# Splitting the last operands by token halves, five sum banks and a new order of the first blocks at the entrance of the up projections of a hybrid decoder on one Trainium2 core

## Chip, cores and metric

The kernel runs on one core of a Trainium2 chip, as a single program. The core has a matrix engine (PE, with its weight loads listed as PEld), a vector engine (DVE), an activation engine (ACT), a general engine (POOL) and a queue that issues transfers (SP). The metric is the device time in microseconds (us), the median of several runs.

## The reference

A decoder of two layers works on 1040 tokens (16 learned meta tokens and 1024 others) of width 1024, in float32. Layer 0 has an SSD mixer, layer 1 stick-breaking attention. After each mixer comes the same gated feed-forward part, and the change lies where the two meet:

```python
h = h + hg @ w_out                     # layer 0: end of the mixer
h = h + o @ sb_w_o[j]                  # layer 1: end of the attention
h = h + _conv_ffn(_rmsnorm(h, ffn_norm[layer]), ...)

def _conv_ffn(u, w_up, conv_w, conv_b, w_down):
    h = _causal_dwconv(u @ w_up, conv_w, conv_b)      # 1024 -> 2 * 2816, three taps
    g, val = jnp.split(h, 2, axis=-1)
    return (jax.nn.silu(g) * val) @ w_down
```

## The kernel before

**Layout.** Activations lie with features on the 128 partitions and tokens along the free dimension: the stream `h` is eight tiles of 128 x 1040. Such wide tiles come from one pool of 28 buffers (`self.Q`, `NQ = 28`, line 25 to 27). A second pool holds twelve short buffers (`ft`, line 756), a third eight (`tmp`). The eight PSUM banks belong to four names: `mm` 2, `sm` 3, `lg` 2, `ex` 1.

**Products.** A float32 product is made of three passes over a high and a low part (`mm3`, line 150): high by high, high by low, low by high. So each operand is split first: ACT copies the high part, and DVE (activations, `split`, line 157) or POOL (weights, `load_w`, line 135) subtracts it to get the low part. `split` does a wide tile in three pieces of 348, 348 and 344 tokens, and its two results take two wide buffers.

**Entrance of the feed-forward part.** `out_proj` (layer 0) and `o_proj` (layer 1) add the mixer's product to `h`. All but the last four operands (layer 0), or the last two (layer 1), are added over the whole rows first; in layer 1 the operands 4 and 5 are added there for the first half of the tokens only. The rest goes through `enter_ffn` (line 714), in four token tiles of 260: `tile(j)` makes eight sums (`accumulate`, line 363: PE into a PSUM bank, then DVE adds the bank to `h`). Their banks are `mm`, `mm`, `ex` in turn, three in all. After tiles 0 and 1 come the factors of the norm for them (`factors`: squares on ACT, sums on POOL and DVE, a product with ones on PE, then Ln, Exp and four instructions of DVE). The weights of the last operands lie partly in the buffers `fh` and `fl` (two each) which the up projection's weights use too.

**Forms.** The up projection is a Winograd variant of Strassen's scheme with seven products in place of eight, over two token tiles at a time: a token pair `t` is 520 tokens (t = 0: tiles 0 and 1; t = 1: tiles 2 and 3). `forms` (line 759) makes its seven operands from the normed `h`, for k = 0 to 3: four scalings on DVE, four subtractions on POOL (all of t = 0; for t = 1 on POOL only where k is 2 or 3, else on DVE), and seven splits (ACT copies, DVE subtracts). Each of the seven forms takes two wide buffers, so one token pair takes 14. The forms are made in the order 1, 5, 0, 2, 3, 4, 6.

**Blocks.** `up` (line 821) runs over 22 blocks of 128 gate and 128 value features. `up_weights` (line 793) loads 1 MB for a block and makes its four weight operands f1 to f4 on ACT and POOL: three differences of 1024 columns, one of 512, and four sums of 512. f2 and f3 lie in the two buffers of `fh` and `fl`, f1 and f4 in three of `wh` and `wl`. A block on one token pair is seven products (0, 2, 3, 1, 4, 5, 6) of twelve matmuls each, with the additions between them, the convolution and the gate on ACT and DVE. Block 0 runs on pair 0, while the factors and forms of pair 1 (`rest`) are made, and then on pair 1; from block 1 on the products of both pairs alternate.

**Order.** Outside of two stretches with an order written by hand (the mixer, and PE in the attention) a planner orders each engine's instructions: of those ready by its own estimate of time, the one written first in the program goes first. The order is fixed before the run, and each engine then works through its list.

Of the kernel before, what the change touches and what calls it, by code (L numbers as in the profile page):

```python
# [8 lines left out]
F32 = mybir.dt.float32  # L9
F32R = mybir.dt.float32r  # L10
AF = mybir.ActivationFunctionType
ALU = mybir.AluOpType

P = 128
# [4 lines left out]
L = META + SEQ  # L19
# [5 lines left out]
QW = 1056  # L25
# [5 lines left out]
FN = 260  # L31
HB = 2
# [8 lines left out]
KF = FF // P  # L41
PAIRS = 8
# [26 lines left out]
class Trunk:  # L69
# [87 lines left out]
    def split(self, t, s, eng=None):  # L157

        nc = self.nc
        hi, lo = self.Q(s + "h", F32R), self.Q(s + "l", F32R)  # L160
        for s0, n in TT:
            c = slice(s0, s0 + n)
            nc.scalar.activation(hi[:, c], t[:, c], AF.Copy)
            (eng or nc.vector).tensor_tensor(lo[:, c], t[:, c], hi[:, c].bitcast(F32), op=ALU.subtract)
        return hi, lo

    def ln_exp(self):
# [192 lines left out]
            self.nc.gpsimd.tensor_copy(t[:, :front], self.zero[:, :front])  # L360
        return t

    def accumulate(self, h, f, s0, n, w, ks, front=0, bank=None):

        ps = (bank or (self.ex if f % 3 == 2 else self.mm))("acc")
        c, o = slice(s0, s0 + n), slice(front + s0, front + s0 + n)
        for i, (hi, lo) in enumerate(ks):
            wh, wl = w(i, f)
            self.mm3(ps[:, :n], wh, wl, hi[:, c], lo[:, c], i == 0, i == len(ks) - 1)
        self.nc.vector.tensor_tensor(h[f][:, o], h[f][:, o], ps[:, :n], op=ALU.add)  # L370
# [324 lines left out]
    def out_proj(self, hd, ys, yd, pool):  # L695

        a = self.a
        h = [None] * KD
        for g in range(3):
            ops = [self.split(ys[g][q] if yd[g] is None else self.fetch(yd[g][q], "y"), "y") for q in range(4)]  # L700
            for f in range(KD):
                w = self.load_w(a["w_out_f"][g, f], 4 * P)
                if g == 0:
                    h[f] = self.fetch(hd[f], "h", front=HB)
                for s0, n in TT:
                    self.accumulate(h, f, s0, n, lambda i, f: (w[0][:, i * P : i * P + P], w[1][:, i * P : i * P + P]), ops, HB)
        ops = [self.split(ys[3][q], "y") for q in range(4)]
        ws = [self.load_wd(a["w_out"][12 + i], pool if i < 2 else None) for i in range(4)]
        return self.enter_ffn(0, h, [(ws, ops)] * 2, pool)

    def load_wd(self, src, pool):
        return self.load_w(src, D, pool=pool, tags=("fh", "fl") if pool else ("wh", "wl"))
# [1 line left out]
    def enter_ffn(self, layer, h, last, pool):  # L714


        nc = self.nc
        r = self.rp.tile([P, QW], F32, tag="r", name=self.nm("r"))
        nc.gpsimd.tensor_copy(r[:, :HB], self.zero[:, :HB])
        d = self.dp.tile([KD, P, L], F32, tag=f"hm{layer}", name=f"hm{layer}")  # L720
        def sums_of(j):
            c = slice(HB + FN * j, HB + FN * j + FN)
            return self.square_sum([x[:, c] for x in h], FN, D), r[:, c]

        def tile(j, work):
            ws, ops = last[j // 2]
            for f in range(KD):
                self.accumulate(h, f, FN * j, FN, lambda i, f: (ws[i][0][:, f * P : f * P + P], ws[i][1][:, f * P : f * P + P]), ops, HB)
                if f % 2:
                    next(work, None)  # L730

        def factors(j):
            sums, c = sums_of(j)
            self.rstd(sums, FN, D, c, j % 2 == 0)

        def rest():
            for j in (2, 3):
                factors(j)
            for k in range(KD):
                nc.sync.dma_start(d[k], h[k][:, HB : HB + L])  # L740
            yield from self.forms(h, r, 1, f"ffn_norm{layer}", forms[1], pool)

        forms = [{i: (self.Q("bh", F32R), self.Q("bl", F32R)) for i in (1, 5, 0, 2, 3, 4, 6)} for _ in range(2)]
        for j in (0, 1):
            tile(j, iter(()))
            factors(j)
        w0 = self.up_weights(layer, 0, pool)
        work = self.forms(h, r, 0, f"ffn_norm{layer}", forms[0], pool)
        tile(2, work)
        tile(3, work)  # L750
        for _ in work:
            pass
        return d, w0, forms, rest()
# [67 lines left out]
    def up(self, layer, w0, forms, rest, pool):  # L821

        nc = self.nc
        tt = nc.vector.tensor_tensor
        N = HB + FN
        cw, cb = f"ffn_conv_w{layer}", f"ffn_conv_b{layer}"
        d = self.dp.tile([KF, P, L], F32, tag=f"g{layer}", name=f"g{layer}")

        def block(b, t, w):

            def product(i, ps, start=True):
                wh, wl, c0 = w[i]
                hi, lo = forms[t][i]
                for k in range(KD // 2):
                    c, e = slice(c0 + k * P, c0 + k * P + P), slice(k * FW, k * FW + N)
                    self.mm3(ps[:, :N], wh[:, c], wl[:, c], hi[:, e], lo[:, e], start and k == 0, k == KD // 2 - 1, not start)
                return ps

            def conv(x, i, c):
                o = self.tmp("c")
                self.conv(x, o[:, :FN], FN, 3, HB, lambda q: self.par(cw, (KF * i + b) * 3 + q), self.par(cb, KF * i + b))
                if i == 0:
                    nc.scalar.activation(o[:, :FN], o[:, :FN], AF.Silu)
                return o

            def done(g, v, j):
                tt(g[:, :FN], g[:, :FN], v[:, :FN], op=ALU.mult)
                nc.sync.dma_start(d[b, :, FN * j : FN * j + FN], g[:, :FN])  # L850

            def copy(ps):
                s = self.ft(pool)
                nc.scalar.activation(s[:, :N], ps[:, :N], AF.Copy)
                return s

            add = lambda o, x, y: tt(o[:, :N], x[:, :N], y[:, :N], op=ALU.add)
            x = product(0, self.mm("p"))
            p1 = copy(x)
            yield  # L860
            y = product(2, self.sm("p"))
            add(y, y, p1)
            u2 = copy(y)
            yield
            z = product(3, (self.ex if next(turn) else self.lg)("p"))
            p5 = copy(z)
            add(z, z, u2)
            yield
            g0 = conv(product(1, x, False), 0, 0)
            yield  # L870
            u3 = copy(product(4, y, False))
            add(p5, p5, u3)
            v1 = conv(p5, 1, 1)
            yield
            done(conv(product(5, z, False), 0, 1), v1, 2 * t + 1)
            yield
            done(g0, conv(product(6, y, False), 1, 0), 2 * t)
            yield

        turn = cycle((0, 0, 1))  # L880
        for b in range(KF):
            w = self.up_weights(layer, b, pool) if b else w0
            s, t = (block(b, t, w) for t in range(2))
            if b:
                for _ in zip(s, t):
                    pass
            else:
                next(rest)
                for _ in s:
                    next(rest, None)  # L890
                for _ in t:
                    pass
        return d

    def down(self, layer, gd, hd, pool, after):
# [347 lines left out]
    def o_proj(self, hd, od, pool):  # L1243

        a = self.a
        h = [None] * KD
        first = PAIRS - 2
        ops = [self.split(self.fetch(od[p], "o"), "o") for p in range(first)]
        for f in range(KD):
            w = self.load_w(a["w_o_f"][f], first * P)  # L1250
            h[f] = self.fetch(hd[f], "h", front=HB)
            for j in range(4):
                self.accumulate(h, f, FN * j, FN, lambda i, f: (w[0][:, i * P : i * P + P], w[1][:, i * P : i * P + P]), ops[: first if j < 2 else first - 2], HB)
        ops = ops[first - 2 :] + [self.split(self.fetch(od[p], "o"), "o") for p in range(first, PAIRS)]
        ws = [self.load_wd(a["w_o"][first - 2 + i], pool if i < 2 else None) for i in range(4)]
        return self.enter_ffn(1, h, [(ws[2:], ops[2:]), (ws, ops)], pool)


    def finish(self, h, j):
# [138 lines left out]
```

## Time and profile before

| | us |
|---|---|
| median of three runs | 3160.1 |
| lowest, highest | 3158.3, 3161.78 |
| profiled execution, device time | 3161.37 |
| profiled execution, span of the trace | 3158.9 |

The profile is one execution. Its span runs from the first to the last instruction; the device time of the same execution is 2.5 us longer. In the trace the entrance of layer 0 lies at about 854 to 953 us from the start of the span and that of layer 1 at about 2310 to 2408 us. A row of a timeline gives the start, the time taken, the engine, the line, the operation with what it writes and reads, the count, and in brackets how long the engine stood idle before it and what ended that. In groups, `bh` and `bl` are the high and low parts of the forms, `acc` a bank of sums, `p` a bank of the blocks' products, `fh` and `fl` the parts of f2 and f3.

### The profile page before, as it was taken

The page shows a single profiled execution, that of the slowest core. Times are in us where ns is not written, and L with a number is a line of the kernel's source. Part 1 is how long each engine was busy: PE and PEld are TensorE (multiplying, and loading weights), DVE is VectorE, ACT ScalarE, POOL GpSimd, SP SyncE. Part 2 cuts the span into 40 slices and gives each one's busy share as a digit, 9 for nine tenths or more (in the row PEclk, how much of TensorE's full clock was granted, in tenths as well). Part 3 has the DMA queues.
Part 4 walks back from the last instruction along what each step waited for, and adds up shares of the span by engine and source line. Part 5 has one row for each costly group of instructions (what it writes and reads, how often), then busy time and mean ns, then how long its engine had stood idle before and what let it go on. Part 6 is the DMA issues. An engine that isn't in the chain of part 4 may idle for free.

```text
span 3158.9 us, 58697 instructions
## 1 busy us (share of the span) xinstructions
PE 2898.4 (92%) x22334; PEld 2764.5 (88%) x22334; DVE 2463.4 (78%) x4227; ACT 1572.4 (50%) x3240; POOL 1686.3 (53%) x1457
## 2 busy tenths in 40 slices
PE   5999999989969999998878999999987999999885
PEld 2999898889969999998877888889886999999885
DVE  3677868875398888889898888878769877788895
ACT  2555545543245555563225555656544565554322
POOL 1154444532347666666675444444356766666653
PEclk9999999999989999999988999999998999999998
DMA  3333333323212222262213222222431222234211
GB/s 113 100 98 97 100 92 100 111 62 127 77 68 70 80 81 76 80 214 77 68 55 100 65 64 64 63 65 59 149 107 48 78 80 80 82 122 170 74 48 54
DMA packets 123348, 277.66 MB, mean 88 GB/s; under 512 B 14492, under 2 KB 54044, under 8 KB 123068
## 3 DMA queue, kind: packets, MB, share of 16 engines
q1 hardware_dynamic: 119670, 262.80, 26.8%
q0 software_dynamic: 2800, 8.83, 0.7%
q8 instruction: 176, 2.88, 0.4%
q10 hardware_dynamic: 598, 2.29, 0.2%
q14 instruction: 104, 0.85, 0.1%
HBM read 201.25 MB, written 53.45 MB: 81 GB/s over the span
## 4 chain that ended last, share of the span: by engine, by line
PE 54%; DVE 15%; issue 2%; ACT 1%; POOL 0%; DMA 0%; DVEq 0%; SPq 0%; ACTq 0%; POOLq 0%
PE p L153 9%; PE p L154 9%; PE p L155 9%; PE acc L153 4%; PE acc L154 4%; PE acc L155 4%; PE pj L153 3%; PE pj L154 3%; PE pj L155 3%; PE po L1177 2%; DVE gl L926 2%; PE wT L1163 2%; PE lg L1132 2%; DVE bl L770 1%; DVE h L992 1%
## 5 line engine op out<-in xcount | busy, mean ns | idle before, releaser
L153 PE MATMUL pj<-uh,wh 128*128 128x348 f32 (+2 forms) x1536 | 512.6, 334 | 8.2 <-ACT bk L596 6.0
L154 PE MATMUL pj<-ul,wh 128*128 128x348 f32 (+2 forms) x1536 | 502.7, 327 | 6.7 <-DVE ul L248 6.7
L155 PE MATMUL pj<-uh,wl 128*128 128x348 f32 (+2 forms) x1536 | 498.7, 325 | 0.0
L147 POOL TENSOR_TENSOR wl<-w,wh 128x1024 fp32r<-128x1024 f32 (+2 forms) x108 | 233.9, 2168 | 354.6 <-ACT wh L146 353.9
L154 PE MATMUL p<-bl,fh 128*128 128x262 f32 x1408 | 402.4, 286 | 12.6 <-DVE bl L770 12.6
L153 PE MATMUL p<-bh,fh 128*128 128x262 f32 x1408 | 402.1, 286 | 7.2 <-ACT bh L769 4.9
L153 PE MATMUL acc<-gh,wh 128*128 128x260 f32 x1184 | 346.9, 293 | 64.3 <-DVE p L992 25.8
L155 PE MATMUL p<-bh,fl 128*128 128x262 f32 x1408 | 400.6, 286 | 4.0 <-POOL fl L808 4.0
L808 POOL TENSOR_TENSOR fl<-x,fh 128x1024 fp32r<-128x1024 f32 x88 | 212.0, 2410 | 265.0 <-ACT fh L807 176.9
L154 PE MATMUL acc<-gl,wh 128*128 128x260 f32 x1184 | 338.4, 286 | 0.0
L155 PE MATMUL acc<-gh,wl 128*128 128x260 f32 x1184 | 337.5, 286 | 0.0
L153 PE MATMUL p<-bh,wh 128*128 128x262 f32 x1056 | 304.6, 288 | 11.5 <-ACT bh L769 11.5
L154 PE MATMUL p<-bl,wh 128*128 128x262 f32 x1056 | 302.9, 287 | 6.8 <-DVE bl L770 6.8
L153 PEld LDWEIGHTS pj<-uh,wh 128*128 128x128 f32 x1536 | 295.7, 193 | 13.2 <-ACT bk L596 6.5
L154 PEld LDWEIGHTS pj<-ul,wh 128*128 128x128 f32 x1536 | 295.9, 193 | 10.0 <-DVE ul L248 8.4
L155 PE MATMUL p<-bh,wl 128*128 128x262 f32 x1056 | 302.1, 286 | 0.0
L270 DVE SCALAR_TENSOR_TENSOR c<-p,params,c 128x260 f32<-128x260 f32 x528 | 251.3, 484 | 58.3 <-ACT c L267 49.3
L153 PEld LDWEIGHTS acc<-gh,wh 128*128 128x128 f32 x1184 | 228.1, 193 | 78.3 <-DVE h L992 28.3
L155 PEld LDWEIGHTS pj<-uh,wl 128*128 128x128 f32 x1536 | 295.3, 192 | 0.2
L154 PEld LDWEIGHTS p<-bl,fh 128*128 128x128 f32 x1408 | 268.2, 190 | 14.1 <-DVE bl L770 13.9
L153 PEld LDWEIGHTS p<-bh,fh 128*128 128x128 f32 x1408 | 267.6, 190 | 8.3 <-ACT bh L769 5.5
L155 PEld LDWEIGHTS p<-bh,fl 128*128 128x128 f32 x1408 | 267.8, 191 | 4.4 <-POOL fl L808 4.4
(277 smaller groups left out, 8496.9 us busy)
## 6 DMA issues: line engine op xcount, KB each, us to landing
w<-in_w_up SPq DMA_DIRECT2D x88, 512.0 KB
g<-c SPq DMA_DIRECT2D x176, 130.0 KB
w<-in_w_down SPq DMA_DIRECT2D x44, 512.0 KB
b<-g SPq DMA_DIRECT2D x40, 520.0 KB
w<-in_w_in SPq DMA_DIRECT2D x40, 512.0 KB
E<-ea_d SPq DMA_DIRECT2D x32, 464.0 KB
D<-acs_d SPq DMA_DIRECT2D x32, 420.5 KB
qs<-qs SPq DMA_DIRECT2D x96, 87.0 KB
```

Of the source, the lines that this page charges most:

```text
L147: nc.gpsimd.tensor_tensor(wl[:, :n], w32[:, :n], wh[:, :n].bitcast(F32), op=ALU.subtract)
L153: mm(out, wh, uh, start=first, stop=False, skip_group_check=joins)
L154: mm(out, wh, ul, start=False, stop=False, skip_group_check=joins)
L155: mm(out, wl, uh, start=False, stop=last, skip_group_check=joins)
L270: nc.vector.scalar_tensor_tensor(out, ps[:, o + i : o + i + n], wcol(i), out, op0=ALU.mult, op1=ALU.add)
L770: nc.vector.tensor_tensor(lo, x, hi.bitcast(F32), op=ALU.subtract)
L808: tt(lo[:, :n], t, hi[:, :n].bitcast(F32), op=ALU.subtract)
L926: tt(lo, x, hi.bitcast(F32), op=SUB)
L992: tt(x, x, ps, op=ADD)
L1132: nc.tensor.matmul(ps[:nt, :m], part[:, c0 : c0 + nt], ks[a][:, s0 : s0 + m], start=x == 0, stop=x == 1)
L1163: nc.tensor.transpose(pt[:ns, x * CB : x * CB + nt], bt[a][:nt, x * CB : x * CB + ns], self.ident[:nt, :nt])
L1177: nc.tensor.matmul(po[64 * a : 64 * a + 64, :nt], v[: CH[c][1], c, 64 * a : 64 * a + 64], wt[a][: CH[c][1], c, :nt], start=x == 0, stop=x ...
```

## The change

1. `split_half` is new: it splits one token half (520 tokens) with one ACT and one DVE instruction, into one wide buffer that holds both parts. In layer 0 the last four operands are split so, first all four for the first half, then all four for the second. In layer 1 operands 4 and 5 are loaded and split for the first half ahead of the whole-row sums, and 6 and 7 for the first half and 4 to 7 for the second half after them; 0 to 3 stay whole. `accumulate` takes the half's first token as `base`.
2. The sums of `enter_ffn` use five banks in turn: `mm`, `lg`, `ex`, `mm`, `lg`.
3. `up` runs block 0 on pair 0, then block 1 on pair 0 and on pair 1, then block 0 on pair 1, then the blocks 2 to 21 on both pairs as before. The weights of block 0 are loaded and made a second time for its second pair. `rest` is drawn from in step with block 0's first pair, as before.

```diff
+    def split_half(self, t, s):
+        x = self.Q(s, F32R)
+        hi, lo = x[:, : L // 2], x[:, QW // 2 : QW // 2 + L // 2]
+        self.nc.scalar.activation(hi, t, AF.Copy)
+        self.nc.vector.tensor_tensor(lo, t, hi.bitcast(F32), op=ALU.subtract)
+        return hi, lo
...
-    def accumulate(self, h, f, s0, n, w, ks, front=0, bank=None):
+    def accumulate(self, h, f, s0, n, w, ks, front=0, bank=None, base=0):
...
-        c, o = slice(s0, s0 + n), slice(front + s0, front + s0 + n)
+        c, o = slice(s0 - base, s0 - base + n), slice(front + s0, front + s0 + n)
...
-        ops = [self.split(ys[3][q], "y") for q in range(4)]
+        ops = [[self.split_half(ys[3][q][:, L // 2 * x : L // 2 * (x + 1)], "y") for q in range(4)] for x in range(2)]
...
-        return self.enter_ffn(0, h, [(ws, ops)] * 2, pool)
+        return self.enter_ffn(0, h, [(ws, o) for o in ops], pool)
...
+        banks = cycle((self.mm, self.lg, self.ex, self.mm, self.lg))
...
-        for b in range(KF):
-            w = self.up_weights(layer, b, pool) if b else w0
-            s, t = (block(b, t, w) for t in range(2))
-            if b:
-                for _ in zip(s, t):
-                    pass
-            else:
+        for n, (b, ts) in enumerate([(0, (0,)), (1, (0, 1)), (0, (1,))] + [(b, (0, 1)) for b in range(2, KF)]):
+            w = self.up_weights(layer, b, pool) if n else w0
+            units = [block(b, t, w) for t in ts]
+            if n == 0:
                 next(rest)
-                for _ in s:
-                    next(rest, None)
-                for _ in t:
-                    pass
+            if n == 1:
+                units = [chain(*units)]
+            for _ in zip(*units):
+                next(rest, None)
...
+        def half(p, x):
+            t = self.Q("o")[:, : L // 2]
+            self.nc.sync.dma_start(t, od[p, :, L // 2 * x : L // 2 * (x + 1)])
+            return self.split_half(t, "o")
+
+        ops = [self.split(self.fetch(od[p], "o"), "o") for p in range(first - 2)]
+        ops = [ops + [half(p, 0) for p in (first - 2, first - 1)], ops]
...
+        ops = [half(p, 0) for p in range(first, PAIRS)], [half(p, 1) for p in range(first - 2, PAIRS)]
...
-        return self.enter_ffn(1, h, [(ws[2:], ops[2:]), (ws, ops)], pool)
+        return self.enter_ffn(1, h, [(ws[2:], ops[0]), (ws, ops[1])], pool)
```

More of the change, by code (lines that the diff above doesn't have):

```diff
@@ L727, in tile @@
             for f in range(KD):
-                self.accumulate(h, f, FN * j, FN, lambda i, f: (ws[i][0][:, f * P : f * P + P], ws[i][1][:, f * P : f * P + P]), ops, HB)
+                self.accumulate(h, f, FN * j, FN, lambda i, f: (ws[i][0][:, f * P : f * P + P], ws[i][1][:, f * P : f * P + P]), ops, HB, next(banks), L // 2 * (j // 2))
                 if f % 2:
@@ L1247, in o_proj @@
         first = PAIRS - 2
-        ops = [self.split(self.fetch(od[p], "o"), "o") for p in range(first)]
+        def half(p, x):
[4 more added lines that the diff above has]
+        ops = [ops + [half(p, 0) for p in (first - 2, first - 1)], ops]
         for f in range(KD):
@@ L1252, in o_proj @@
             for j in range(4):
-                self.accumulate(h, f, FN * j, FN, lambda i, f: (w[0][:, i * P : i * P + P], w[1][:, i * P : i * P + P]), ops[: first if j < 2 else first - 2], HB)
-        ops = ops[first - 2 :] + [self.split(self.fetch(od[p], "o"), "o") for p in range(first, PAIRS)]
+                self.accumulate(h, f, FN * j, FN, lambda i, f: (w[0][:, i * P : i * P + P], w[1][:, i * P : i * P + P]), ops[j // 2], HB)
+        ops = [half(p, 0) for p in range(first, PAIRS)], [half(p, 1) for p in range(first - 2, PAIRS)]
         ws = [self.load_wd(a["w_o"][first - 2 + i], pool if i < 2 else None) for i in range(4)]
-        return self.enter_ffn(1, h, [(ws[2:], ops[2:]), (ws, ops)], pool)
+        return self.enter_ffn(1, h, [(ws[2:], ops[0]), (ws, ops[1])], pool)
     def finish(self, h, j):
```

## The prediction

> **What bounds the kernel now.** I read the page first, then the busy times by stretch, then the waits and the timelines of the two places where the product engine thins out.
>
> ```profile
> span 3158.9 us, 58697 instructions
> PE 2898.4 (92%) x22334; PEld 2764.5 (88%) x22334; DVE 2463.4 (78%) x4227; ACT 1572.4 (50%) x3240; POOL 1686.3 (53%) x1457
> ```
>
> PE is the bound over the whole, so what counts is where it stands still. The stretches below (start:end, length, busy of PE, PEld, DVE, ACT, POOL with counts, clock, DMA share, GB/s) are the entrance of layer 0, six rows, and of layer 1, four rows.
>
> ```profile
> 854.00:889.00 35.00, 35.00 (x286) 34.56 (x284) 21.17 (x48) 12.84 (x29) 11.25 (x12) 1.00 0.11 32
> 889.00:909.00 20.00, 14.12 (x105) 12.90 (x105) 20.00 (x42) 12.08 (x29) 11.04 (x15) 1.00 0.41 167
> 909.00:926.00 17.00, 8.41 (x39) 6.95 (x37) 16.79 (x13) 6.25 (x16) 16.92 (x11) 0.62 0.24 87
> 926.00:953.00 27.00, 14.87 (x80) 12.86 (x79) 26.28 (x64) 15.06 (x38) 6.67 (x9) 0.67 0.07 19
> 953.00:1000.00 47.00, 46.03 (x364) 45.85 (x365) 39.62 (x62) 26.96 (x56) 34.78 (x20) 0.96 0.25 80
> 1000.00:1400.00 400.00, 400.00 (x3294) 400.00 (x3293) 325.07 (x516) 235.35 (x478) 266.08 (x150) 1.00 0.30 97
> ```
>
> ```profile
> 2310.00:2342.00 32.00, 32.00 (x263) 31.77 (x262) 19.86 (x50) 12.62 (x27) 15.02 (x12) 1.00 0.21 67
> 2342.00:2363.00 21.00, 14.00 (x93) 12.77 (x93) 21.00 (x43) 12.00 (x31) 12.53 (x16) 0.92 0.30 120
> 2363.00:2382.00 19.00, 8.14 (x42) 6.05 (x41) 18.83 (x16) 8.02 (x19) 18.92 (x14) 0.79 0.24 93
> 2382.00:2408.00 26.00, 14.32 (x80) 12.58 (x80) 25.38 (x62) 14.57 (x37) 6.54 (x9) 0.69 0.07 21
> ```
>
> From 1000 to 1400 PE never stops: 400/3294 = 0.1214 us per matmul. Against that rate the 224 matmuls from 889 to 953 are 27.2 us of work in 64, and the 215 from 2342 to 2408 are 26.1 in 66. So about 37 and 40 us are lost, 77 in all, and there DVE is full (20.00, 16.79 and 26.28 of 20, 17 and 27). The entrances are DVE's. Ahead of 889 PE is full, so there is no late split of the last operands to be seen, only what they occupy.
>
> Why DVE is slow there is in its groups by shape, the first three from 908 to 927, the next from 854 to 953, the last four from 953 to 1000 (behind the bar: busy us, mean ns).
>
> ```profile
> L770 DVE TENSOR_TENSOR bl<-ft,bh 128x262 fp32r<-128x262 f32 x9 | 13.1, 1493 | 0.0
> L219 DVE TENSOR_TENSOR sq<-sq,sq 128x260 f32<-128x260 f32 x3 | 4.1, 1364 | 0.2
> L370 DVE TENSOR_TENSOR h<-h,acc 128x260 f32<-128x260 f32 x1 | 0.4, 411 | 0.0
> ```
>
> ```profile
> L777 DVE TENSOR_TENSOR ft<-b,ft 128x262 f32<-128x262 f32 x6 | 2.6, 425 | 0.0
> ```
>
> ```profile
> L270 DVE SCALAR_TENSOR_TENSOR c<-p,params,c 128x260 f32<-128x260 f32 x26 | 12.2, 483 | 2.5 <-ACT c L267 2.3
> L849 DVE TENSOR_TENSOR c<-c,c 128x260 f32<-128x260 f32 x8 | 10.0, 1256 | 0.2
> L857 DVE TENSOR_TENSOR ft<-ft,ft 128x262 f32<-128x262 f32 x6 | 6.8, 1131 | 0.0
> L857 DVE TENSOR_TENSOR p<-p,ft 128x262 f32<-128x262 f32 x10 | 4.1, 432 | 2.3 <-ACT ft L854 1.5 <-PE p L155 0.7
> ```
>
> Operations that take one input from PSUM (acc, p) cost 0.41 to 0.48 us whatever POOL does; those with both inputs in SBUF cost 1.1 to 1.5 while POOL is at work and 0.42 (the L777 row, whose six stand between 934 and 943, where POOL is idle). In 909 to 926 POOL is busy 16.92 of 17, with the weights of blocks 0 and 1; an operation of DVE then costs up to 1.49 - 0.42 = 1.07 us more.
>
> **The change, part by part.** Three rows of the timelines show what the token halves free: PE's last sum, ACT just behind it, and ACT at the same place of layer 1.
>
> ```profile
> 908.07 0.28 PE L155 MATMUL acc<-yh,wl 128*128 128x260 f32 x1
> ```
>
> ```profile
> 909.05 1.03 ACT L769 ACTIVATE bh<-ft 128x262 fp32r<-128x262 f32 x3
> ```
>
> ```profile
> 2363.69 1.03 ACT L769 ACTIVATE bh<-ft 128x262 fp32r<-128x262 f32 x3
> ```
>
> The pool of wide buffers has 28: eight rows h and eight split operands leave 12, but the forms of one token pair want 14. The seventh form waits until the last sum has read the operands, and then three of its parts come at once. With halves, four buffers are free after the second token tile (28 - 8 - 4 = 16), and these parts go ahead of POOL's burst. Each saves up to 1.07 us on DVE: three are 3.2, all nine of the group above 9.6, none if DVE, already full before 909, only shifts its work. I take 3 per entrance, the count that the ACT row names. The splits themselves become 16 instructions for 24 under a full PE, and layer 1 issues four more DMAs on SP, whose issues take 0.32 us (row below) while PE is full (32.00 of 32 before 2342): nothing; uncovered, four of them are 1.3 us.
>
> ```profile
> 2257.72 0.32 SPq L358 DMA_DIRECT2D o<-o_d  x1
> ```
>
> Five banks answer this wait (layer 0, from 885 to 955; below it layer 1, from 2338 to 2410; total us, times, longest):
>
> ```profile
> PE acc L153 <- DVE h L370: 5.9, 5, 1.6
> ```
>
> ```profile
> PE acc L153 <- DVE h L370: 5.8, 4, 2.1
> PE p L153 <- ACT bh L769: 8.2, 2, 5.7
> PE p L154 <- DVE bl L770: 11.5, 6, 4.3
> ```
>
> PE would end its sums up to 6 us sooner, but what follows needs DVE's additions, and DVE is full. The stall only moves to the products: 0 from this alone, at the most 5.9.
>
> The order of blocks is the large part. The products of block 0 stop at the second pair's forms:
>
> ```profile
> 932.17 0.59 PE L153 MATMUL p<-bh,wh 128*128 128x262 f32 x1 [5.81 <-ACT bh L769]
> 953.11 0.39 PE L154 MATMUL p<-bl,fh 128*128 128x262 f32 x1 [0.95 <-DVE bl L770]
> ```
>
> Block 1 on the first pair puts seven products of twelve matmuls, 84 x 0.1214 = 10.2 us, into that gap, and later PE has them behind it, since from 953 on PE is the bound (46.03 of 47). Above: all 10.2. Below: 0, if DVE's full queue keeps their banks. Four of the seven (the first three and the one that follows on the first bank) want only ACT's copies: 48 x 0.1214 = 5.8. DVE's idle fifth in the next stage (400 - 325 of 400) pays back the rest over some 40 us. I take 8.
>
> Making block 0's weights again costs one MB on SP's queue (DMA share 0.25: hidden), four ACT copies (hidden, ACT 235 of 400) and POOL's work, whose price is in the steady rows, 1000 to 1400:
>
> ```profile
> L808 POOL TENSOR_TENSOR fl<-x,fh 128x1024 fp32r<-128x1024 f32 x37 | 89.0, 2405 | 119.2 <-ACT fh L807 75.2 <-PE p L155 44.0
> L808 POOL TENSOR_TENSOR wl<-w,wh 128x1024 fp32r<-128x1024 f32 x18 | 46.6, 2586 | 0.0
> L815 POOL TENSOR_TENSOR x<-w,w 128x512 f32<-128x512 f32 x18 | 24.6, 1364 | 1.4
> L808 POOL TENSOR_TENSOR wl<-w,wh 128x512 fp32r<-128x512 f32 x18 | 23.3, 1294 | 0.1
> ```
>
> 2 x 2.4 + 2.6 + 1.3 + four sums of 1.3 to 1.4 are 14 us a block (the sums by the L815 row). POOL's slack after 953 is 47 - 34.8 = 12.2 us, so nearly all fits, but POOL is then full for some 45 us and each of the five SBUF operations that DVE has per block and pair loses a few tenths more, 1 to 2 us over three pairs; and between the second pair of block 0 (10.2 us of PE) and block 2, POOL has 14 to make. Bounds 0 and -14; I take -3, nearer the slack. One more: block 1's second operand is wanted in the gap itself, and its difference (2.4 us) then holds DVE's forms; two or three such are 2 to 5. I take -2.5. What is late next is DVE, not PE: its 5.9 us for block 1's first pair (6 x 0.48, 2 x 0.43 and five SBUF operations at 0.42) queue behind the forms.
>
> The Trainium skill, "SBUF — State Buffer", section "Who interferes with whom", says that a vector instruction with two SBUF inputs and a GpSimd one that reads SBUF lock each other out for the whole instruction. The rows agree (1493 against 411 ns). By the rule alone, each microsecond that POOL gains where DVE is the bound is one lost, 14 per entrance in place of the 3, and the sum would be 11 the other way, 3171; the first rival is that case, worked out from rows.
>
> **The sum**, per entrance: 3 + 8 - 3 - 2.5 = 5.5 us, 11 in both. The profiled execution took 3161.4 us (span 3158.9, 2.5 around it), 1.3 over the median of 3160.1. 3161.4 - 11 = 3150.4, at the median 3149.
>
> **Rivals.** POOL becomes the bound (slower). Left of block 1 are its second, third and fourth operand (6.1 us), then 14 and 14: 34 us of POOL for the 30.6 us (252 matmuls) of PE in block 1 and block 0's second pair. That is 3.4 us of PE's waiting; three long differences among the forms hold DVE 2 us each beyond its 0.42, 6 more; with no lead won and the 3 of the early buffers kept, 6.4 per entrance are lost, 13 in both: 3173. It decides from the point where block 1's operands cannot be begun before about 940, since the two buffers of each weight part come free only with block 0's products. For it: POOL 34.78 of 47 already. Against: POOL idles from 926 to 943, as its next row there says.
>
> ```profile
> 943.90 0.75 POOL L777 TENSOR_TENSOR ft<-b,ft 128x262 f32<-128x262 f32 x1 [17.70 <-ACT bh L769]
> ```
>
> Nothing moves: DVE finishes the forms at the same time, and the lead is given back as PE waits for its banks or because the planner's order still puts the second pair's products first, as at 932 it did ahead of block 0's own: within 6 us, 3160. For it: DVE at 26.28 of 27.
>
> The whole gap is filled: 10.2 and the upper part of the buffers, 7 per entrance, 34 in all: 3126. For it: 77 us are lost, this is under half. Against: nothing of DVE's work is taken away.
>
> **How the numbers follow.** About 0.2% (6.3 us) is what a measurement of this kernel can tell from no change; its three runs lie 3.5 us apart. The forecast 0.42 (3139 to 3154), the filled gap 0.15, nothing 0.16, POOL 0.27. Faster 0.57, same 0.16, slower 0.27. The likeliest's own range is 3139 to 3154; with the other cases 3128 to 3174, which leaves out half of the filled gap and a part of the POOL case.
>
> **What would show it.** Right: matmuls in the 64 us behind the last full stretch rise from 224 to about 290; the three seventh-form copies stand ahead of the last sum; the waits of sums for h go to about 1 us. Wrong: the same stretch longer than 64 us, products waiting for fl of L808 or for c of L267 in the 50 us after it, or the first pair of block 1 behind the second pair's forms in PE's order.

## The result, and the profile after

| | before | after |
|---|---|---|
| median, us | 3159.72 | 3174.05 |
| lowest, highest, us | 3158.3, 3161.78 | 3170.2, 3177.4 |
| profiled execution, device time, us | 3161.37 | 3171.36 |
| span of its trace, us | 3158.9 | 3169.6 |

The ratio is 1.0048, with an interval from 1.0036 to 1.006: the change makes the kernel slower by about 14 us, where 11 less were forecast. One execution of e8_dummy (12723 us) and one of e11_once (3309 us) further down fell into a far slower state and are left out of their medians.

The page of the changed kernel, its first rows:

```profile
span 3169.6 us, 58706 instructions
...
PE 2905.0 (92%) x22334; PEld 2769.3 (87%) x22334; DVE 2486.9 (78%) x4219; ACT 1576.2 (50%) x3240; POOL 1718.6 (54%) x1473
```

PE has the same 22334 matmuls. POOL has 16 instructions and 32.3 us more, the second making of block 0's weights twice. DVE has eight instructions fewer and is yet busy 23.5 us longer (2463.4 before): the same work takes it longer.

The stretches of the changed kernel (start:end, length, busy of PE, PEld, DVE, ACT, POOL, clock, DMA share, GB/s); three rows from the entrance of layer 0, three from that of layer 1:

```profile
880.00:898.00 18.00, 16.72 (x135) 15.89 (x133) 18.00 (x39) 9.46 (x25) 9.32 (x11) 1.00 0.22 88
898.00:921.00 23.00, 9.06 (x35) 6.94 (x35) 22.86 (x24) 10.75 (x22) 22.77 (x18) 0.62 0.36 141
921.00:963.00 42.00, 26.14 (x122) 22.79 (x123) 37.22 (x67) 19.21 (x46) 18.48 (x16) 0.70 0.09 26
...
2348.00:2359.00 11.00, 9.70 (x78) 9.08 (x77) 11.00 (x26) 5.76 (x17) 4.80 (x6) 1.00 0.34 138
2359.00:2384.00 25.00, 8.82 (x36) 6.86 (x34) 23.34 (x28) 11.90 (x26) 24.21 (x18) 0.68 0.36 135
2384.00:2424.00 40.00, 25.63 (x123) 22.69 (x124) 36.68 (x68) 19.03 (x47) 18.38 (x16) 0.71 0.07 25
```

Layer 0: 292 matmuls from 880 to 963, 35.4 us of work at 0.1214 us each, in 83 us. Layer 1: 237 from 2348 to 2424, 28.8 us in 76. Lost are 47.6 and 47.2 us, 95 in all, where it was 77 before: 18 more. The loss is in the entrances, and the last rows of both show where: POOL, which worked 6.67 of 27 us in the stretch of pair 1's forms before, now works 18.48 of 42.

The forms of pair 1 on DVE, from the last norm factor (`r`) to the last low part (`bl`), in the timeline before:

```profile
930.39 0.43 DVE L186 TENSOR_TENSOR r<-r,sq 128x260 f32<-128x260 f32 x1
...
931.66 2.50 DVE L774 SCALAR_TENSOR_TENSOR b<-h,params,r 128x262 f32<-128x262 f32 x6
...
949.05 4.34 DVE L770 TENSOR_TENSOR bl<-ft,bh 128x262 fp32r<-128x262 f32 x7
...
953.66 0.42 DVE L770 TENSOR_TENSOR bl<-ft,bh 128x262 fp32r<-128x262 f32 x1
```

and after (the lines are eight or nine higher):

```profile
927.89 0.43 DVE L194 TENSOR_TENSOR r<-r,sq 128x260 f32<-128x260 f32 x1
...
929.16 6.64 DVE L783 SCALAR_TENSOR_TENSOR b<-h,params,r 128x262 f32<-128x262 f32 x6
...
953.12 8.64 DVE L779 TENSOR_TENSOR bl<-ft,bh 128x262 fp32r<-128x262 f32 x7
...
962.37 0.41 DVE L779 TENSOR_TENSOR bl<-ft,bh 128x262 fp32r<-128x262 f32 x1
```

From factor to last low part it was 23.3 us and is 34.5. The same six scalings take 6.64 in place of 2.50 us, the same seven differences 8.64 in place of 4.34: 8.4 of the 11.2. What POOL does meanwhile, after:

```profile
928.94 2.51 POOL L817 TENSOR_TENSOR fl<-x,fh 128x1024 fp32r<-128x1024 f32 x1 [7.58 <-ACT fh L816]
931.53 1.34 POOL L821 TENSOR_TENSOR x<-w 128x512 f32<-128x512 f32 x1
932.96 1.35 POOL L822 TENSOR_TENSOR x<-x,w 128x512 f32<-128x512 f32 x1
943.85 1.27 POOL L817 TENSOR_TENSOR wl<-w,wh 128x512 fp32r<-128x512 f32 x1 [9.55 <-ACT wh L816]
...
956.12 2.52 POOL L817 TENSOR_TENSOR fl<-x,fh 128x1024 fp32r<-128x1024 f32 x1
958.72 1.33 POOL L824 TENSOR_TENSOR x<-w,w 128x512 f32<-128x512 f32 x1
960.01 1.46 POOL L825 TENSOR_TENSOR x<-w,x 128x512 f32<-128x512 f32 x1
```

Seven instructions of weight work, 11.8 us, stand among the forms: three are differences of block 1's weights (6.3 us), four are sums of block 0's second making (5.5 us). Before, POOL's first weight work after the burst (its work on the weights of blocks 0 and 1 from 909 to 926) came at 957.63, when the last low part (953.66) was done; the row of POOL's timeline before names its releaser, ACT's copy:

```profile
957.63 2.40 POOL L808 TENSOR_TENSOR fl<-x,fh 128x1024 fp32r<-128x1024 f32 x1 [5.55 <-ACT fh L807]
```

After, this subtraction begins 28.7 us earlier (928.94). ACT's copy ahead of it, in its timeline of the changed kernel, waits for a product of PE, the reader that lets go of the buffer:

```profile
927.81 1.06 ACT L816 ACTIVATE fh<-x 128x1024 fp32r<-128x1024 f32 x1 [1.11 <-PE p L154]
```

So the new order brings the weight work forward. Before, block 0's second pair still needed its weights, so their buffers came free only after pair 1's forms; now block 0's products of pair 0 are the last to read them. The buffers come free sooner, and POOL starts the next weights in the very stretch where its idleness had let DVE run.

### The profile page after: what moved, and what is told of

Same layout as the page of the kernel before. It is cut to its first block, busy times and chain, and to the rows that moved or that the text cites. A ratio compares the mean times of both kernels' runs of the same rounds, so it can differ in the third digit from the quotient of the medians.

```text
span 3169.6 us, 58706 instructions
## 1 busy us (share of the span) xinstructions
PE 2905.0 (92%) x22334; PEld 2769.3 (87%) x22334; DVE 2486.9 (78%) x4219; ACT 1576.2 (50%) x3240; POOL 1718.6 (54%) x1473
## 4 chain that ended last, share of the span: by engine, by line
PE 68%; DVE 19%; issue 4%; POOL 3%; ACT 2%; DMA 2%; SPq 0%; DVEq 0%; POOLq 0%; ACTq 0%
PE p L153 8%; PE p L154 8%; PE p L155 8%; PE pj L153 6%; PE pj L154 6%; PE pj L155 6%; PE acc L153 5%; PE acc L154 5%; PE acc L155 5%; PE po L1184 2%; DVE gl L933 2%; PE wT L1170 2%; PE lg L1139 2%; DVE bl L779 2%; DVE h L999 1%
## 5 line engine op out<-in xcount | busy, mean ns | idle before, releaser
L817 POOL TENSOR_TENSOR fl<-x,fh 128x1024 fp32r<-128x1024 f32 x92 | 224.0, 2435 | 246.8 <-ACT fh L816 176.4
```

The costliest lines, as they stand in the source:

```text
L817: tt(lo[:, :n], t, hi[:, :n].bitcast(F32), op=ALU.subtract)
```

## The experiments

All times are medians of five rounds beside the kernel before on the same chip. That kernel took 3156.6 to 3158.6 us in the experiments and 3159.7 in the result's own run, so the ratios compare better than the times. The expectations call PE also TensorE, DVE VectorE, ACT ScalarE and POOL GpSimd. The table gives, for each entrance (layer 0, then layer 1), four lengths in us, worked out from the start times of four rows of each trace: from the first matmul of the mixer's output sums (710.48 in layer 0 before) to the last norm factor ("factor"); from there to the last low part of pair 1's forms ("forms"); from there to the 1008th matmul of the blocks, twelve units of 84 ("rest"); and their sum. Each length hangs on one execution, so differences of 1 us or so should not be read.

| kernel | time | ratio, interval | factor | forms | rest | sum |
|---|---|---|---|---|---|---|
| before | 3159.7 | | 219.9, 127.1 | 23.3, 23.7 | 110.7, 111.4 | 353.9, 262.3 |
| after | 3174.1 | 1.0048 [1.0036, 1.006] | 222.5, 127.3 | 34.5, 34.0 | 108.1, 108.3 | 365.1, 269.6 |
| e1_halves | 3158.7 | 1.0 [0.9991, 1.0008] | 219.8, 128.5 | 23.2, 23.2 | 110.7, 111.2 | 353.8, 263.0 |
| e2_banks | 3158.5 | 1.0 [0.999, 1.0009] | 220.8, 128.5 | 23.2, 23.3 | 109.9, 110.0 | 353.9, 261.8 |
| e3_halves_banks | 3156.3 | 0.9996 [0.9988, 1.0005] | 221.6, 127.3 | 23.3, 23.3 | 109.9, 110.8 | 354.7, 261.4 |
| e4_order | 3174.9 | 1.0052 [1.004, 1.0064] | 220.9, 127.2 | 33.0, 33.3 | 108.1, 108.2 | 362.0, 268.7 |
| e6_pool1 | 3149.4 | 0.998 [0.9971, 0.9988] | 217.4, 122.9 | 23.4, 25.7 | 111.7, 107.4 | 352.6, 255.9 |
| e6_pool2 | 3174.2 | 1.0055 [1.0042, 1.0067] | 223.3, 127.3 | 30.4, 29.2 | 110.7, 111.4 | 364.4, 267.9 |
| e6_pool12 | 3149.0 | 0.9973 [0.9964, 0.9982] | 218.1, 122.3 | 23.5, 24.4 | 112.2, 111.8 | 353.7, 258.4 |
| e7_defer | 3155.4 | 0.9996 [0.9987, 1.0005] | 216.1, 122.4 | 23.5, 23.5 | 112.8, 115.4 | 352.5, 261.3 |
| e8_dummy | 3169.5 | 1.0046 [1.0033, 1.006] | 220.7, 127.4 | 29.5, 27.3 | 112.0, 110.0 | 362.2, 264.7 |
| e9_old_pool1 | 3142.3 | 0.9959 [0.9946, 0.9971] | 214.2, 120.8 | 23.2, 23.3 | 109.1, 109.7 | 346.6, 253.7 |
| e10_wq | 3141.6 | 0.996 [0.9947, 0.9972] | 211.5, 123.3 | 23.3, 23.3 | 109.7, 110.2 | 344.5, 256.8 |
| e10b_wq_order | 3158.6 | 1.0005 [0.9996, 1.0014] | 215.3, 126.9 | 29.8, 28.8 | 107.9, 108.3 | 353.0, 264.0 |
| e11_once | 3169.2 | 1.0039 [1.0026, 1.0052] | 222.4, 127.3 | 34.5, 34.0 | 105.7, 106.2 | 362.6, 267.5 |
| e12_once_pool1 | 3138.8 | 0.9936 [0.9925, 0.9948] | 217.0, 122.8 | 23.5, 23.4 | 106.4, 106.4 | 346.8, 252.7 |
| e13_wq_only | 3147.5 | 0.9962 [0.995, 0.9974] | 213.7, 123.8 | 23.3, 23.3 | 110.2, 109.8 | 347.1, 256.8 |

The table's main reading: the rest lies between 105.7 and 112.8 us but for one length (115.4), whatever the kernel. Factor and forms carry most of the differences, so what mainly decides the time is when the last low part of pair 1 is ready. Both lengths end with work of DVE.

**The parts one by one.** The halves alone:

```diff
...
-        ops = [self.split(ys[3][q], "y") for q in range(4)]
+        ops = [[self.split_half(ys[3][q][:, L // 2 * x : L // 2 * (x + 1)], "y") for q in range(4)] for x in range(2)]
...
```

> Token halves alone (three banks, old order of blocks). Theory P (POOL's weights of block 1 and of the second block 0 hold DVE's forms of pair 1): nothing of that is here, so 3154 to 3160 us, the 3 us per entrance that the early buffers were to give or none. Rival E (the earlier end of the sums lets POOL's burst for blocks 0 and 1 fall on more of DVE's forms and square sums): here already part of the loss, 3163 to 3168. Three seventh-form copies of ACT should stand ahead of the last sum.

The five banks alone:

```diff
...
+        banks = cycle((self.mm, self.lg, self.ex, self.mm, self.lg))
...
-                self.accumulate(h, f, FN * j, FN, lambda i, f: (ws[i][0][:, f * P : f * P + P], ws[i][1][:, f * P : f * P + P]), ops, HB)
+                self.accumulate(h, f, FN * j, FN, lambda i, f: (ws[i][0][:, f * P : f * P + P], ws[i][1][:, f * P : f * P + P]), ops, HB, next(banks))
...
```

> Five banks alone. Theory P: no effect, 3157 to 3163 us, with the waits of the sums for h (5.9 us before) gone and as much more waiting at the products. Rival E: the sums end some 6 us sooner, the burst too, 3163 to 3168.

Both:

> Halves and five banks, old order of blocks, weights made once. Theory P: 3150 to 3158 us, the loss is all in the order of blocks. Rival E: 3165 to 3172, most of the loss of the whole change.

The new order with the second making, on the kernel before:

```diff
...
-        for b in range(KF):
-            w = self.up_weights(layer, b, pool) if b else w0
+        for n, (b, ts) in enumerate([(0, (0,)), (1, (0, 1)), (0, (1,))] + [(b, (0, 1)) for b in range(2, KF)]):
+            w = self.up_weights(layer, b, pool) if n else w0
...
```

> The new order of blocks with block 0's weights made twice, alone. Theory P: it carries the loss, 3170 to 3182 us, and DVE's forms of pair 1 take some 8 us longer per entrance than before. Rival E: 3156 to 3164, as the sums end where they did.

3158.7, 3158.5, 3156.3 and 3174.9. This is as theory P of these texts has it, and rival E is out: the halves and the banks are worth nothing that can be told, and the whole loss belongs to the order with its second making. The banks did what they say; the waits of the changed kernel, 875 to 905 (total us, times, longest; 5.9 in five before):

```profile
PE acc L153 <- DVE h L378: 1.1, 1, 1.1
```

The sums end 6 us sooner in layer 0 (191.4 us after their first matmul in e3_halves_banks, 197.6 before), but the last norm factor does not (221.6 and 219.9).

**Which of POOL's work.** In the changed kernel POOL's subtractions and sums for the weights of one making become ScalarE copies, so the low parts and sums hold other values. First block 1's, `n in (1,)`; then block 0's second making, `n in (2,)`; then both:

```diff
...
-        tt = nc.gpsimd.tensor_tensor
+        tt = (lambda o, x, y, op: nc.scalar.activation(o, x, AF.Copy)) if act else nc.gpsimd.tensor_tensor
...
-            w = self.up_weights(layer, b, pool) if n else w0
+            w = self.up_weights(layer, b, pool, n in (1,)) if n else w0
...
```

> The changed kernel, but block 1's differences and sums of weights are ACT copies in place of POOL's work (its values are other ones). Theory P (POOL's weight work inside the forms of pair 1 holds DVE): second and third difference and burst of block 1 gone, 8 to 12 us per entrance less, 3150 to 3160 us. Rival S (the second making, 14 us of POOL in 47, is what costs, later on): little, 3168 to 3174. Rival O (PE's order with block 1 in between, and DVE's longer queue, cost whatever POOL does): 3168 to 3176.

> The changed kernel, but the second making of block 0's weights takes ACT copies in place of POOL's differences and sums (other values). Theory P: its four sums stood inside the forms (two of them at 931, two at 958), 3 to 5 us per entrance less, 3162 to 3168 us. Rival S: all the loss gone, 3150 to 3160. Rival O: 3170 to 3176.

> The changed kernel with ACT copies for both, block 1 and the second making (other values). Theory P: the loss is gone and the lead that block 1 was to give is seen, 3138 to 3152 us. Rival S: the same as the run with the second making alone, 3150 to 3160. Rival O: 3166 to 3176.

3149.4, 3174.2, 3149.0. Taking POOL's work for block 1 away gives 25 us, which speaks against the rivals S and O. Taking its work for the second making away gives nothing, where theory P expected 6 to 12 us: the forms become 4 to 5 us shorter (30.4 and 29.2), but the rest is about 3 longer (110.7 and 111.4). ACT's copies in place of POOL's work may be the reason; no run shows it. DVE's rows in e6_pool1, the six scalings and the seven differences:

```profile
928.29 2.50 DVE L783 SCALAR_TENSOR_TENSOR b<-h,params,r 128x262 f32<-128x262 f32 x6
...
945.51 4.35 DVE L779 TENSOR_TENSOR bl<-ft,bh 128x262 fp32r<-128x262 f32 x7
```

2.50 and 4.35 us again, as before the change. But this run also made block 1's weights ready sooner, so it leaves two readings: POOL holds DVE, or PE waits for POOL's weights.

**Putting the weight work off.** The old order with halves and banks, where two one-column copies on POOL bind block 1's weights to a late form of pair 1, so that the old order's burst loses its share for block 1:

```diff
...
+        if gate is not None:
+            for x in (g, v):
+                nc.gpsimd.tensor_copy(x[:, :1], gate)
...
```

> Old order of blocks, halves and five banks, and block 1's loads wait (through two columns that POOL copies) for the third quarter of pair 1's forms, so that POOL's six operations for block 1 no longer stand among the square sums. Theory P: 4 to 8 us per entrance less than halves and banks alone (3156), 3140 to 3150 us, unless block 1's weights are then late, 3150 to 3160. Rivals S and O: 3156 or slower by the later weights, 3154 to 3164.

3155.4, no difference. The last factor is 5.5 and 4.9 us sooner than in e3_halves_banks, so the burst holds the squares too; the rest is 2.9 and 4.6 longer. That block 1's weights are then late is likely, but not shown: in the rest PE's listed waits for weights are 0.7 us in either entrance. The run loses in the one what it wins in the other and does not tell the two readings apart.

**Holding without lateness.** This one does: as e6_pool1, with POOL doing the same operations into a tile that nobody reads.

```diff
...
+        def both(o, x, y, op):
+            nc.scalar.activation(o, x, AF.Copy)
+            for s in range(0, o.shape[1], H):
+                nc.gpsimd.tensor_tensor(act[:, H:], x[:, s : s + H], y[:, s : s + H], op=op)
+
+        tt = nc.gpsimd.tensor_tensor if act is None else both
...
```

> The changed kernel with block 1's split weights (the low parts and the four sums of both entrances) written by ScalarE copies, so that TensorE never waits for them on GpSimd, while GpSimd still does the same subtractions and additions at the same places, into a tile nobody reads (the 1024-wide ones as two of 512). The values of block 1's low parts and sums are thus others than the reference's. Theory H (GpSimd's work at this place holds VectorE's forms of pair 1, and late forms are what the time is lost to): the forms of pair 1 take about 34 us again from the last norm factor to the last low half, and the time is 3168 to 3175, ratio 1.003 to 1.0055. Theory L (block 1's weights came late for TensorE because GpSimd made them late; the long forms are only beside it): 3149 to 3153, ratio 0.9973 to 0.999, with the forms still at about 34 us. Anything between, 3155 to 3166, would mean that both share the loss.

3169.5: of the 25 us that e6_pool1 had won, 20 are back (by the ratios 0.66 of 0.68 per cent), though no split weight of block 1 is made by POOL here. POOL's rows of this run from the time of pair 1's forms (933.52 is a sum, 937.87 a difference), and below them DVE's:

```profile
933.52 4.28 POOL L826 TENSOR_TENSOR x<-w 128x512 f32<-128x512 f32 x1 [3.71 <-ACT bh L778]
937.87 1.35 POOL L827 TENSOR_TENSOR x<-x,w 128x512 f32<-128x512 f32 x1
...
953.38 2.79 POOL L810 TENSOR_TENSOR wl<-x,fh 128x512 fp32r<-128x512 f32 x2 [0.76 <-ACT fh L821]
```

```profile
933.85 1.79 DVE L779 TENSOR_TENSOR bl<-b,bh 128x262 fp32r<-128x262 f32 x5
...
938.00 1.91 DVE L783 SCALAR_TENSOR_TENSOR ft<-h,params,r 128x262 f32<-128x262 f32 x2
...
949.58 4.01 DVE L779 TENSOR_TENSOR bl<-ft,bh 128x262 fp32r<-128x262 f32 x6
```

The holding goes both ways: the 512-wide sum, 1.34 us in the changed kernel (931.53), takes POOL 4.28 here, where DVE's differences run at their full pace (1.79 us for five). The forms are 29.5 and 27.3 us, shorter than the 34 that was expected, and the last factor is 3.3 and 4.5 us later than in e6_pool1; together they are the 9.4 and 6.1 us by which the last low part is late. That POOL holds DVE, and that this costs the time, is shown. What is left between this run and the changed kernel, 5 us by the medians, 8 by the sums and next to nothing by the ratios, can be lateness of the weights or the longer forms there. The waits of PE in the changed kernel, from 897 to 963 (total us, times, longest), leave little for lateness:

```profile
PE p L153 <- ACT bh L778: 12.4, 6, 6.3
PE p L154 <- DVE bl L779: 10.0, 5, 4.2
PE p L155 <- POOL fl L817: 2.8, 2, 1.8
```

PE stands 22.4 us for the forms and 2.8 for low parts of the weights from POOL. One thing e8_dummy does not hold apart: POOL's copy of the work also reads the weights' sources, so these buffers come free later than in e6_pool1. The rest, where that would be seen, is 0.3 and 2.6 us longer.

**The old order without that work.**

```diff
...
-            w = self.up_weights(layer, b, pool) if b else w0
+            w = self.up_weights(layer, b, pool, b in (1,)) if b else w0
...
```

> The order of before, with the halves and the five banks, and block 1's low parts and sums by ScalarE copies instead of GpSimd's subtractions and additions (other values than the reference's). With the changed order the same replacement gave 3149.4, ratio 0.998. If the new order is worth something by itself once GpSimd is out of its way (the 8 us that the prediction gave it for each entrance), this run stays 5 to 16 us behind that one: 3154 to 3166, ratio 0.9997 to 1.003. If the order is worth nothing, or costs something even without GpSimd, it is level with it or ahead: 3140 to 3150, ratio 0.995 to 0.998.

3142.3, 7 us ahead of the new order with the same replacement. In the old order POOL's work for block 1 lies in the burst, over the square sums: without it the last factor is 7.4 and 6.5 us sooner than in e3_halves_banks, with no change in the forms. The same cost is thus there in the old order, smaller, one stage earlier.

**A version that keeps the work and moves it.** The first two of the last four weights of the sums go into wide buffers in place of `fh` and `fl`, so that block 0's f2 and f3 are made while the sums still run:

```diff
-        ws = [self.load_wd(a["w_out"][12 + i], pool if i < 2 else None) for i in range(4)]
+        ws = [self.load_wq(a["w_out"][12 + i]) if i < 2 else self.load_wd(a["w_out"][12 + i], None) for i in range(4)]
...
+    def load_wq(self, src):
+        nc = self.nc
+        w32 = self.wp.tile([P, 1024], F32, tag="w32", name=self.nm("w32"))
+        nc.sync.dma_start(w32, src)
+        wh, wl = (self.Q("wq", F32R)[:, :D] for _ in range(2))
+        nc.scalar.activation(wh, w32, AF.Copy)
+        nc.gpsimd.tensor_tensor(wl, w32, wh.bitcast(F32), op=ALU.subtract)
+        return wh, wl
```

(and the same for `w_o`). With halves and banks in the old order; with the whole change; and alone on the kernel before:

> The order of before, with the halves and the five banks, and of the last four weights of the sums ahead of each entrance the first two go into wide buffers, so that block 0's third and fourth up weights find their own buffers free earlier and GpSimd makes these and the sums of block 1 before the burst. If the entrance is bound by what GpSimd still has to do after the last sums (H and L alike), it falls by 3 to 8 us for each entrance: 3143 to 3152, ratio 0.995 to 0.998. If the wide buffers are then missing for the first split parts, which are the first operands of the entrance, it is level or slower: 3156 to 3166.

> The changed kernel with the first two of the last four weights in wide buffers as in the run before. If GpSimd's weight work among the forms of pair 1 is what costs the new order its time, and this takes two of its subtractions out of it, 3155 to 3166 (ratio 0.9985 to 1.002); if it does not reach that stretch, as before 3171 to 3176.

> The kernel before with the first two of the last four weights of the sums in wide buffers, without the halves and without the five banks. If the gain of 15 us came from the weights alone: 3139 to 3145, ratio 0.995 to 0.9965. If the earlier end of the sums is part of it once GpSimd no longer binds: 3147 to 3155, ratio 0.997 to 0.9995.

3141.6, 3158.6 and 3147.5: ratios 0.996, 1.0005 and 0.9962. The first beats both kernels, by 15 us the one before. POOL's rows of e10_wq show what is left of the burst:

```profile
905.44 1.45 POOL L826 TENSOR_TENSOR wl<-w,wh 128x512 fp32r<-128x512 f32 x1
906.85 0.92 POOL L795 TENSOR_TENSOR ft<-ft,ft 128x262 f32<-128x262 f32 x1
907.74 2.53 POOL L826 TENSOR_TENSOR wl<-w,wh 128x1024 fp32r<-128x1024 f32 x1
...
933.36 0.76 POOL L795 TENSOR_TENSOR ft<-b,ft 128x262 f32<-128x262 f32 x1 [19.55 <-ACT bh L787]
```

Two weight differences, where the burst had filled 16.92 of 17 us before, and then POOL is idle for 19.55 us while DVE makes the forms in 23.3. The last factor comes 10.1 us sooner in layer 0 than in e3_halves_banks and 4.0 in layer 1. With the new order on top (e10b_wq_order) the forms take 29.8 and 28.8 and 14 (by the ratios) to 17 us are lost again. e13_wq_only takes 6 us more than e10_wq, but on another chip; the ratios, 0.9962 and 0.996, tell no difference, so what the halves and banks add here stays open.

**What the second making and the order itself are worth.** Block 0's second pair is multiplied with block 1's weights (other values for it), so nothing is made twice; once on the changed kernel, once with e6_pool1's replacement too:

```diff
...
-            w = self.up_weights(layer, b, pool) if n else w0
+            w = w if n == 2 else self.up_weights(layer, b, pool) if n else w0
...
```

> The changed kernel without the second making: block 0's second token pair is multiplied with block 1's weights, which stand in SBUF at that point, so seven weight parts fewer are loaded, copied and differenced for each entrance (block 0's values of pair 1 are others than the reference's). If the second making costs what the prediction gave it, 3 us for each entrance, or more by its loads and ScalarE copies: 3160 to 3169, ratio 1.001 to 1.004. If it costs nothing, as leaving out GpSimd's part of it alone did: 3171 to 3176, ratio 1.0045 to 1.006.

> As the run before, and block 1's low parts and sums by ScalarE copies in place of GpSimd's work: the new order with neither GpSimd's work among the forms nor a second making. If TensorE's order is free, or gains by filling the gap, and the 7 us behind the old order came from the second making: 3138 to 3144, ratio 0.9945 to 0.9965. If the order itself costs them: 3147 to 3152, ratio 0.997 to 0.9985.

3169.2 and 3138.8. Beside POOL's hold the second making costs little: 3 us by the ratios (1.0039 against 1.0048, whose intervals overlap), 2.5 and 2.1 in the table's sums. This lies at the edge between the two expectations. The forms are as long as in the changed kernel (34.5 and 34.0), for in e11_once the next block's sums stand in the place of the second making's. Without the hold it costs more: 3138.8 against e6_pool1's 3149.4, and 5.8 and 3.2 us in the sums. In both of these runs block 1's weights are made by ACT's copies, so this is not the price in the changed kernel. The order itself gains: the rest is 105.7 to 106.4 us in these two runs against 109.1 to 110.8 in e9_old_pool1 and e3_halves_banks. A row of PE in e12_once_pool1 shows why it is no more:

```profile
932.78 0.59 PE L153 MATMUL p<-bh,fh 128*128 128x262 f32 x1 [9.19 <-ACT bh L778]
```

With block 1's weights ready and POOL quiet, PE still stands 9.19 us before the first form of pair 1. Ahead of this row PE has 72 matmuls of the blocks, where the kernel before has 36 ahead of its wait at 932.17: only three of block 1's seven products are in PE's list ahead of pair 1's. The sums of e12_once_pool1 and e9_old_pool1 (346.8 and 252.7; 346.6 and 253.7) are level; of the 3.5 us between their medians (7 by the ratios) the entrances explain 1, and the rest stays open.

## Why the prediction was wrong

**What bounds the kernel: right.** The entrances are DVE's, and POOL's hold on its two-input operations lengthens them.

**Halves, 3 per entrance: nothing.** The mechanism came: in e1_halves three copies of pair 0's forms stand behind the last sum (909.18, 911.32 and 912.25, the sum at 906.72), where six did before. But the table's sums (353.8 and 263.0 for e1_halves, 353.9 and 262.3 before) do not move. That is the lower bound that the prediction gave, DVE's work only shifted. **Banks, 0: right**, and the way too: in e2_banks the stall goes from 5.9 to 1.1 us, and PE's waits for DVE's `bl` and `sq` from 9.9 to 18.2 (850 to 1000).

**Block 1 on the first pair, 8 per entrance: a gain, mis-sized.** From e3_halves_banks to e11_once, the change without the second making, the rest shrinks by 4.2 and 4.6 us. "Four of the seven" were counted to go into the gap; PE's list has three there (36 matmuls, 4.4 us at 0.1214).

**Second making, 3: about 2**, by e11_once. Nothing like the 14 of POOL's full work on it is lost.

**The step that failed** is "its difference (2.4 us) then holds DVE's forms; two or three such are 2 to 5. I take -2.5." It is 11.2 and 10.7 us by the forms of e3_halves_banks and the changed kernel. This term alone turns the sign of the forecast. It counted two or three differences at 1 to 2 us each. What counts is all that the freed buffers let POOL do among the forms, the seven instructions shown, and nearly at their full length (11.8 us). Behind it stands a misreading: "POOL idles from 926 to 943" was held against the first rival, as room for POOL's work. That idleness was what let the six scalings take 2.50 us.

By the measured terms the sum is 0 + 4.4 - 2.3 - 11 = -8.9 per entrance, 18 in both. The sums of the table say 18.5 (11.2 and 7.3), the profiled spans 10.7, the medians 14. The trace of after starts the entrance of layer 0 5.1 us earlier (705.4 for 710.5), in work that the change doesn't touch; why is not known.

**The rival "POOL becomes the bound"** gave 3173 and the measurement is 3174, but that its number fits is luck: only its direction and half of its reasons held. It had 6 us of hold, 3.4 us of PE's waiting and no lead, and kept 3 us of the early buffers; the runs show 11 of hold, a lead of 4.4, nothing for the buffers, and little lateness of weights (2.8 us of PE's waits for `fl`).

**The signs named beforehand.** Matmuls in the 64 us behind the last full stretch were to rise from 224 to about 290 (the three rows of the prediction count some twice; in one row they are 220). PE is now full until 890. One row of before and one of after, in the columns named above:

```profile
889.00:953.00 64.00, 37.40 (x220) 32.70 (x219) 63.07 (x117) 33.40 (x82) 34.63 (x33) 0.76 0.22 83
```

```profile
890.00:954.00 64.00, 37.69 (x187) 31.82 (x186) 59.09 (x100) 29.60 (x68) 37.54 (x32) 0.71 0.24 92
```

They fell to 187. "The same stretch longer than 64 us" was a sign of wrong, and it came. Another, products waiting for `fl` or `c` in the 50 us after it, did not: from 963 to 1013 PE waits 0.4 us in all. The seventh form's copies were to stand ahead of the last sum. ACT's timeline of the changed kernel, the first and the last of six single copies of pair 0's forms behind that sum (897.65):

```profile
898.50 0.42 ACT L778 ACTIVATE bh<-ft 128x262 fp32r<-128x262 f32 x1 [0.53 <-POOL ft L786]
...
910.55 0.41 ACT L778 ACTIVATE bh<-ft 128x262 fp32r<-128x262 f32 x1
```

Before there were six as well, three of them at once at 909.05: no three come at once any more, but the five banks end the sums sooner too, and seven of these differences on DVE still lie in the burst (898 to 921), where nine did (908 to 927).

## What to carry to other kernels

When one engine bounds a stage and a helper's work holds its operations, as POOL's does DVE's here, the helper's idle time in that stage is no free capacity; its work there is paid in the bound engine's time, instruction by instruction. When an order is changed to fill a gap, list what each buffer that comes free earlier releases on every engine, and at which point of the bound engine's work this falls. Where such work can't be dropped, bring it ahead of the stage: here other buffers for two weights gave 11 to 15 us.

## What the runs showed of the hardware

One instruction of POOL lets about one two-input instruction of DVE through. The first of the six scalings, in the changed kernel's timeline from 928 to 930:

```profile
929.16 2.58 DVE L783 SCALAR_TENSOR_TENSOR b<-h,params,r 128x262 f32<-128x262 f32 x1
```

It starts 0.22 us into POOL's 2.51 us difference (928.94) and ends at 931.74, 0.29 behind its end; with POOL idle one takes about 0.42 (2.50 for six). Two more end 0.3 behind the two POOL instructions that follow, and the last three run freely: six of them beside three POOL instructions of 5.2 us took 6.64. The Trainium skill, "SBUF — State Buffer", section "Who interferes with whom", describes this as an exclusive lock for the whole instruction, and these rows agree. What was not expected is how far it decides a whole entrance: the last low part is 9.4 and 6.1 us later in e8_dummy than in e6_pool1, with the same products, for work whose result nobody reads. That POOL pays for it as well (4.28 in place of 1.34 us) had not been expected either.
